# Adaptive visits in the stick-breaking stage: four weight tiles at every second gate tile, with other buffers and first loads

## The chip, the cores and the metric

The kernel runs on one core of one Trainium2 chip. The core has a matrix engine (TensorE, PE in the profile), a vector engine (VectorE, DVE), a scalar engine (ScalarE, ACT), GpSimd (POOL) and SyncE (SP), which here only issues loads. Sixteen DMA engines move data between the chip's memory and the on-chip SBUF; PE writes its sums into eight banks of PSUM. Each engine works through its own instructions in order and waits on semaphores for the others. The metric is the device time of one execution in microseconds.

## The reference

One step of an encoder layer, for a prompt of 1024 rows and a sample of 32 rows with 512 cached rows:

```python
ada = jax.nn.silu(c) @ w_ada + b_ada
sh1, sc1, gt1, sh2, sc2, gt2 = [a[:, None, :] for a in jnp.split(ada, 6, axis=-1)]
h = rms_norm(x, g_pre_mix) * (1 + sc1) + sh1
q_nope, q_rope, c_kv, k_rope, q_b, k_b, v_b, g_a, g_b = mixer_inputs(h, pos, w_in, g_q_lat, w_uq, g_kv_lat)
...
o_a = sweep_query_blocks(mla_attend, (q_nope, q_rope), pos, (k_nope, k_rope, v_a), pos)
o_b = sweep_query_blocks(sb_attend, (q_b,), pos, (k_b, v_b), pos)
...
merged = (g_a * (o_a.reshape(B, T, H_A * DV) @ w_proj_a)
          + g_b * (o_b.reshape(B, T, H_B * D_HB) @ w_proj_b))
x = x + gt1 * rms_norm(merged @ w_out, g_post_mix)
h2 = rms_norm(x, g_pre_ffn) * (1 + sc2) + sh2
f, new_conv = conv_ffn(h2, conv_state, w_up, conv_w, conv_b, w_down)
x = x + gt2 * rms_norm(f, g_post_ffn)
```

`sb_attend` is the stick-breaking attention: a score matrix, a softplus, a cumulative sum from the right, an exponential, and the product with the values, strictly causal. The adaptive product `silu(c) @ w_ada` has two rows on its left side (prompt and sample) and 1024 x 6144 weights. Its first two sixths are needed for `h`, at the start; the other four (gate 1, shift 2, scale 2, gate 2) only later.

## The kernel before

The stages run one after the other: `stage_h` (norm, first two sixths of the adaptive product), `stage_qkv`, `stage_sb` (stick-breaking attention), `stage_lat` and `stage_mla` (latent attention), `stage_merge`, `stage_up`, `stage_down`. The change lies in `stage_sb` (line 1106) and what it calls.

**The stage.** Four passes, `p` = 0 to 3, each over one pair of heads. What PE, ACT and DVE do in a pass, and in which order, is written out by hand in the string `ORDER`; the loop of `sb_attend` (line 713) reads it token by token, and the order of the tokens is the order on each engine. `S` is a block of scores on PE into a PSUM bank (`S2.0a`: query pair 2, first of two, part a; pairs 0 to 3 are the first head, 4 to 7 the second). `a`, `e`, `l` and `E` are ACT's absolute value, exponential, logarithm and last exponential; `x`, `c`, `k` and `d` are DVE's maximum and sum, cumulative sum, copy and difference. `d` is the last to read the bank, which a later `S` takes over; there are three such banks. `T` turns finished blocks on PE, `h` (ACT) and `v` (DVE) split them into a high and a low part, `V` multiplies them with the values on PE, `o` and `p` bring the result out.

**What fills PE.** The sixteen weight tiles of gates A and B run in between (`gates`, line 1043), four in each pass. A gate tile is three blocks of 352 columns; a block is eight steps, and the token `f` is one step (three matmuls, lines 75 to 77). `G` copies a finished block out of its bank (ACT, line 1080, two buffers `nat`), and GpSimd stores it (line 1081). `W` (ACT) and `w` (DVE) split the next tile's weights, which SP loads when a tile begins.

**The adaptive product.** The last four sixths are 32 weight tiles of 128 x 1024. `ada_step` (line 228) is a visit: for each of `n` tiles four matmuls (line 236), each into 32 rows of one PSUM bank of the tag `mm`, that the gates use too. Before, `n` is 2, and a visit stands behind the first block of each gate tile, as two further `f` steps: sixteen visits, four a pass, which are called the first to the fourth visit here. In the third of a pass a score block, `S6.1b`, stands between the two tiles. The visit's sum is added to an accumulator on DVE (line 244, token `D`), and the next two tiles are fetched (`ada_fetch`, line 218) into the pool `att` (`self.sm2`, tag `A`, five buffers). After eight tiles a sixth is complete: PE turns it (`ada_turn`, line 250) behind the second block of the gate tile, and token `Q` puts it away. The very first two tiles are fetched at the start of the stage into the pool `sb` (`S`), between the loads of the first head's Q and K and those of its V.

**Queues.** All loads of the stage go through SP in the order of the program: `load` (line 83) chains each to the one before. Behind the first loads come the next gate tile's weights (`wr`), then the second head's Q and K (token `S2.0a`), its V (`S2.1a`), and from `S3.1b` and `V3.0` on those of the next pass. The caches of the sample rows (`sample_load(1)`) are loaded at the last gate tile. Stores and the bias rows of the adaptive product go through GpSimd.

Of the kernel before, what the change touches and what calls it, by code (L numbers as in the profile page):

```python
# [8 lines left out]
F32 = mybir.dt.float32  # L9
# [8 lines left out]
P = 128  # L18
D = 1024
KT = 8  # L20
TP = 1024
# [11 lines left out]
BIG = 1056  # L33
# [11 lines left out]
class K:  # L45
# [182 lines left out]
    def ada_step(self, n, pool, tp, late):  # L228


        nc, a = self.nc, self.a
        ps = self.bank("mm")
        for i, (v, k) in enumerate(self.ada_todo[:n]):
            w = self.ada_w.pop(0)
            for j in range(4):
                nc.tensor.matmul(ps[32 * j : 32 * j + 32, :256], self.cT[:, k], w[:, j * 256 : j * 256 + 256],
                                 start=i == 0, stop=i == n - 1)
            if i < n - 1:
                yield
        if v > 2 and self.ada_todo[0][1] == 0:  # L240
            self.acc = self.tl(tp, [P, 256], F32, "ada")
            self.ada_bias(v)
        acc = self.acc
        late.append(lambda: nc.vector.tensor_tensor(acc, acc, ps[:, :256], ALU.add))
        del self.ada_todo[:n]
        self.ada_fetch(n, pool)
        self.ada_sum = v if k == KT - 1 else None
        yield

    def ada_turn(self):  # L250

# [192 lines left out]
    def stage_qkv(self):  # L444
# [245 lines left out]

    ORDER = """
        S0.0 S0.1 a0.0 S1.0 a0.1 e0.0 e0.1 l0.0 f2 l0.1 x0.0 a1.0 x0.1 f1 c0.1 c0.0 e1.0 f1 l1.0 f1 d0.0 d0.1
        E0.0 f1 x1.0 c1.0 E0.1 f1 S1.1 S2.0a a1.1 T0.0 d1.0 f1 G a2.0a h0.0 v0.0 f1 e2.0a f1 e1.1 S2.0b l2.0a D
        f2 l1.1 x2.0a V0.0 E1.0 c2.0a f1 a2.0b o0 f1 x1.1 e2.0b f1 W p0 f1 k2.0a d2.0a l2.0b f1 c1.1 E2.0a f1
        S2.1a x2.0b G f1 a2.1a d1.1 e2.1a c2.0b f2 E1.1 f1 w l2.1a S2.1b f1 a2.1b x2.1a T1.1 e2.1b T1.0 d2.0b
        h1.1 c2.1a f1 h1.0 f1 l2.1b v1.1 S3.0a E2.0b v1.0 f1 a3.0a f1 k2.1a d2.1a G e3.0a x2.1b V1.1 E2.1a c2.1b
        l3.0a S3.0b V1.0 x3.0a a3.0b o1 f1 p1 T2.2 h2.2 e3.0b d2.1b f1 c3.0a f1 E2.1b f1 l3.0b v2.2 S3.1a k3.0a
        d3.0a T2.1 h2.1 a3.1a x3.0b E3.0a V2.2 f1 c3.0b T2.0 e3.1a S3.1b h2.0 f1 v2.1 l3.1a f1 G v2.0 a3.1b f1
        x3.1a W f1 d3.0b V2.1 c3.1a D V2.0 f1 w o2 S4.0 e3.1b E3.0b f1 a4.0 f1 l3.1b f1 p2 e4.0 k3.1a d3.1a l4.0
        f2 x3.1b E3.1a f1 x4.0 c3.1b f1 G T3.3 c4.0 S4.1 a4.1 T3.2 h3.3 d3.1b f1 e4.1 v3.3 h3.2 f1 d4.0 f1 l4.1  # L700
        E3.1b v3.2 S5.0 f1 E4.0 x4.1 c4.1 a5.0 V3.3 e5.0 V3.2 l5.0 d4.1 T3.1 E4.1 x5.0 T3.0 h3.1 f1 c5.0 h3.0
        S5.1 S6.0a v3.1 a5.1 f1 v3.0 a6.0a T4.0 e5.1 f1 d5.0 h4.0 V3.1 E5.0 v4.0 f1 l5.1 V3.0 G x5.1 S6.0b e6.0a
        f1 o3 c5.1 f1 a6.0b l6.0a e6.0b f1 p3 l6.0b d5.1 f2 x6.0b E5.1 V4.0 x6.0a f1 o4 c6.0a S6.1a T5.1 p4
        a6.1a T5.0 k6.0a d6.0a h5.1 f1 c6.0b e6.1a f1 G h5.0 v5.1 f1 E6.0a v5.0 S6.1b l6.1a f1 W f1 x6.1a d6.0b
        V5.1 V5.0 D c6.1a E6.0b a6.1b S7.0a w o5 f2 e6.1b l6.1b a7.0a f1 k6.1a p5 e7.0a f1 d6.1a x6.1b E6.1a f1
        c6.1b l7.0a S7.0b f1 x7.0a T6.2 a7.0b f1 d6.1b h6.2 c7.0a f1 E6.1b f1 G e7.0b S7.1a v6.2 f1 k7.0a d7.0a
        l7.0b T6.1 T6.0 a7.1a h6.1 V6.2 x7.0b c7.0b h6.0 S7.1b e7.1a f1 v6.1 E7.0a f1 v6.0 l7.1a f1 d7.0b a7.1b
        f1 x7.1a V6.1 E7.0b V6.0 e7.1b c7.1a f1 G o6 l7.1b f1 p6 k7.1a d7.1a x7.1b f2 E7.1a f1 c7.1b f2 T7.3
        d7.1b T7.2 h7.3 f1 h7.2 E7.1b v7.3 f1 G f1 v7.2 f1 V7.3 V7.2 D T7.1 f1 h7.1 v7.1 T7.0 f1 h7.0 v7.0 f1
        V7.1 f2 V7.0 f1 o7 f1 W p7 f1 Q f1 w G f7 G  # L710
    """.split()

    def sb_attend(self, score, V, out, fill, then):
        nc = self.nc
        act, vec = nc.scalar.activation, nc.vector
        tiles, banks, seen = {}, {}, {}
        common = self.sums(V, out, tiles)
        todo = None
        for x in self.ORDER:
            if todo:  # L720
                todo()
            todo = then.get(x)
            k, x = x[0], x[1:]
            if k in "fGDQWw":
                for _ in range(int(x or 1)):
                    fill(k)
                continue
            h, u = divmod(int(x[0]), 4)
            if k in "SaelxckdE":
                n, i, part = x[0], int(x[2]), x[3:]  # L730
                w = (2 * u + i + 1) * P
                m = w // 2 if part else w
                c0 = m if part == "a" else 0
                if k == "S":
                    if part != "b":
                        tiles[x[:3]] = self.tl(self.At, [P, TP], F32, "A")
                    banks[x] = self.tl(self.ps, [P, 512], F32, "s")
                    score(h, banks[x], 2 * u + i, c0, max(m, 256))
                    continue
                ps, A = banks[x][:, :m], tiles[x[:3]][:, c0 : c0 + m]  # L740
                if k == "a":
                    act(A, ps, AF.Abs)
                elif k == "e":
                    act(A, A, AF.Exp, scale=-1.0)
                elif k == "l":
                    act(A, A, AF.Ln, bias=1.0)
                elif k == "x":
                    vec.scalar_tensor_tensor(A, ps, 0.0, A, ALU.max, ALU.add)
                elif k == "c":
                    r = A[:, ::-1]  # L750
                    if part == "b":
                        vec.tensor_tensor_scan(r, r, r, seen[x[:3]], ALU.add, ALU.bypass)
                    else:

                        vec.tensor_tensor_scan(r, self.reset[:, 512 - m : 512][:, ::-1], r, -NEG, ALU.mult, ALU.add)
                elif k == "k":
                    seen[x[:3]] = self.tl(self.sm, [P, 1], F32, "mn")
                    vec.tensor_copy(seen[x[:3]], A[:, 0:1])
                elif k == "d":
                    vec.tensor_tensor(A, ps, A, ALU.subtract)  # L760
                else:
                    act(A, A, AF.Exp)  # L762
                continue
            common(k, x, h, u)
# [278 lines left out]
    def gates(self):  # L1043
# [7 lines left out]
        def steps():  # L1051
            for m in range(16):
                wh, wl = w.pop(0)
                for b, (c0, n) in enumerate(self.BLK):
                    if b == 0:
                        c = 2208 + (m + 1) * P if m < 15 else 3 * P
                        raw.append(self.wload([(0, 1024, self.a["w_in"][0, :, c : c + P].rearrange("(k p) c -> p k c", p=P), 8)]))
                    ps.append((m, c0, n, self.bank("mm")))
                    for k in range(KT):
                        self.mm3(ps[-1][3][:, :n], wh[:, k], wl[:, k], self.Hh[k][:, c0 : c0 + n],  # L1060
                                 self.Hl[k][:, c0 : c0 + n], k == 0, k == KT - 1)
                        if k < KT - 1:
                            yield
                    if b == 1 and self.ada_sum is not None:
                        ada.append(self.ada_turn())
                    yield
                    if b == 0:
                        yield from self.ada_step(2, self.sm2, self.Sp, ada)
                        if m == 15:
                            self.sample_load(1)  # L1070

        step = steps()

        def do(kind):
            if kind == "f":
                next(step)
            elif kind == "G":
                m, c0, n, x = ps.pop(0)
                g = self.tl(self.At, [P, 512], F32, "nat")
                nc.scalar.copy(g[:, :n], x[:, :n])  # L1080
                nc.gpsimd.dma_start(self.gd[m, :, c0 : c0 + n], g[:, :n])
            elif kind in "DQ":
                ada.pop(0)()
            elif kind == "W":
                w.append((self.tl(self.W, [P, 1024], F32R, "wh"), self.tl(self.W, [P, 1024], F32R, "wl")))
                self.hi(w[0][0], raw[0])
            else:
                self.lo(w[0][1], raw.pop(0), w[0][0])
                w[0] = tuple(v(x) for x in w[0])
# [16 lines left out]
    def stage_sb(self):  # L1106
# [35 lines left out]
            self.tl(S, [P, TP], F32, "A")  # L1142
        first(0)
        self.sm2 = self.tc.alloc_tile_pool(name="att", bufs=2, reuse_waits="tile")

        self.sent = self.wlast
        queries(0, 0)
        self.ada_w = []
        self.ada_fetch(2, S)
        values(0, 0)  # L1150

        def score(h, ps, i, c0, n):
# [5 lines left out]
        E = mybir.EngineType  # L1158
        for p in range(4):
            then = {"S2.0a": lambda: queries(p, 1), "S2.1a": lambda: values(p, 1)}  # L1160
            if p < 3:
                then.update({"S3.1b": lambda: queries(p + 1, 0), "V3.0": lambda: values(p + 1, 0)})
            with self.tc.manual_schedule(engines={E.PE, E.Activation, E.DVE}):
# [1443 lines left out]
```

## Time and profile before

| What | Value |
|---|---|
| Runs, median (lowest to highest) | 1707.84 us (1705.19 to 1708.3), 3 runs |
| Profiled execution, its own time | 1706.82 us |
| Its span, first to last instruction | 1704.7 us |
| Mean granted PE clock | 0.994 |
| Matmuls of the adaptive visits (line 236) | 256 records, 18.2 us busy |
| DVE additions of the visits (line 244) | 16 of about 0.41 us |

How to read the views: times are microseconds from the span's start. In the timeline a row is start, duration, engine, line, operation, tile written and tiles read, shape and count of merged instructions; a bracket at its end is the idle time of the engine before the row and what ended it. Matmuls are pipelined, so the distance from one start to the next tells what one costs, rather than its duration. An fp32 matmul of a visit leaves two records, so a tile of four matmuls has eight. A row of an SP or POOL DMA is its issue, not the transfer. In a view by stretch there stand, behind the stretch and its length, the busy time and instruction count of each engine, PE's granted clock, the share of the DMA engines' time and the GB/s moved.

### The profile page before, as it was taken

How to read it: one execution, taken by the hardware profiler on the slowest of the kernel's cores; microseconds unless marked ns; L12 is line 12 of the kernel's file. 1: busy time of each engine (PE TensorE's matmuls, PEld its weight loads, DVE VectorE, ACT ScalarE, POOL GpSimd, SP SyncE). 2: the span in 40 equal slices, each digit the busy share in tenths (PEclk: the TensorE clock that was granted, in tenths of full speed). 3: DMA queues.
4: the chain of work that ended last, by engine and by line, in shares of the span. 5: the costliest groups of instructions: out<-in, count | busy, mean ns of one | idle time of the engine just before them, and what ended most of it. 6: DMA issues, size and time to landing. Idle time of an engine off the chain costs nothing. (4 is left out here: it accounts for less than half of the span.)

```text
span 1704.7 us, 30268 instructions
## 1 busy us (share of the span) xinstructions
PE 1660.8 (97%) x11646; PEld 1512.1 (89%) x11646; DVE 1272.9 (75%) x2129; ACT 993.6 (58%) x1945; POOL 292.8 (17%) x569
## 2 busy tenths in 40 slices
PE   5999999999999999999999999999999999999997
PEld 3999889999999898998889789999999999887885
DVE  4865697979783688777766779887787777787456
ACT  4544597978774667777763476444444444544442
POOL 3113311111110221111100221221121111110013
PEclk8999999999999999999999999999999999999999
DMA  9345984647432421222374531433333333697643
GB/s 333 100 133 180 280 250 130 200 117 227 150 104 66 149 79 47 67 68 70 107 238 140 173 131 62 134 104 131 131 104 132 131 108 133 231 331 250 207 139 120
DMA packets 185728, 255.20 MB, mean 150 GB/s; under 512 B 14702, under 2 KB 125056, under 8 KB 185584
## 3 DMA queue, kind: packets, MB, share of 16 engines
q1 hardware_dynamic: 164944, 194.11, 36.5%
q0 software_dynamic: 20416, 59.08, 9.8%
q8 instruction: 91, 1.49, 0.4%
q14 instruction: 53, 0.43, 0.1%
q10 hardware_dynamic: 224, 0.09, 0.0%
HBM read 187.86 MB, written 64.57 MB: 148 GB/s over the span
## 5 line engine op out<-in xcount | busy, mean ns | idle before, releaser
L68 ACT ACTIVATE wh<-wr 128x1024 fp32r<-128x1024 f32 (+5 forms) x163 | 132.2, 820 | 226.3 <-PE s L2061 80.4
L71 DVE TENSOR_TENSOR wl<-wr,wh 128x1024 fp32r<-128x1024 f32 (+5 forms) x163 | 149.9, 928 | 78.0 <-ACT wh L68 77.6
L75 PE MATMUL mm<-hh,wh 128*128 128x352 f32 x456 | 153.0, 336 | 0.0
L76 PE MATMUL mm<-hl,wh 128*128 128x352 f32 x456 | 149.5, 328 | 0.4 <-DVE hl L331 0.3
L77 PE MATMUL mm<-hh,wl 128*128 128x352 f32 x456 | 148.7, 326 | 0.0
L2060 PE MATMUL mm<-T,wh 128*128 128x256 f32 (+1 forms) x376 | 108.1, 288 | 0.0
L2062 PE MATMUL mm<-T,wl 128*128 128x256 f32 (+1 forms) x376 | 107.0, 285 | 0.3 <-DVE wl L71 0.2
L2061 PE MATMUL mm<-T,wh 128*128 128x256 f32 (+1 forms) x376 | 106.7, 284 | 0.0
L2060 PE MATMUL s<-T,wh 128*128 128x256 f32 (+1 forms) x348 | 99.2, 285 | 0.0
L2062 PE MATMUL s<-T,wl 128*128 128x256 f32 (+1 forms) x348 | 99.1, 285 | 0.0
L2061 PE MATMUL s<-T,wh 128*128 128x256 f32 (+1 forms) x348 | 99.0, 284 | 0.0
L71 DVE TENSOR_TENSOR wl<-S,wh 128x1024 fp32r<-128x1024 f32 (+1 forms) x55 | 59.1, 1077 | 49.2 <-ACT wh L68 48.8
L76 PEld LDWEIGHTS mm<-hl,wh 128*128 128x128 f32 x456 | 86.4, 190 | 3.3 <-DVE hl L331 1.8
L75 PEld LDWEIGHTS mm<-hh,wh 128*128 128x128 f32 x456 | 86.4, 190 | 3.2 <-ACT A L762 1.6
L2201 DVE SCALAR_TENSOR_TENSOR u<-u,c,u 128x1058 f32<-128x1058 f32 x68 | 87.0, 1316 | 2.0 <-ACT u L2198 0.7
L77 PEld LDWEIGHTS mm<-hh,wl 128*128 128x128 f32 x456 | 86.5, 190 | 0.2
L803 PE MATMUL tr<-c,A 128*128 128x128 f32 x576 | 84.2, 275 | 0.9 <-DVE A L919 0.3
L68 ACT ACTIVATE wh<-S 128x1024 fp32r<-128x1024 f32 (+1 forms) x55 | 51.8, 943 | 49.5 <-PE s L2061 13.4
L2062 PE MATMUL tr<-T,wl 128*128 128x272 f32 (+1 forms) x272 | 77.6, 285 | 0.2 <-DVE wl L71 0.2
L2060 PE MATMUL tr<-T,wh 128*128 128x272 f32 (+1 forms) x272 | 77.7, 286 | 0.0
L2061 PE MATMUL tr<-T,wh 128*128 128x272 f32 (+1 forms) x272 | 77.3, 284 | 0.0
L71 DVE TENSOR_TENSOR PTl<-tr,PTh 128x512 fp32r<-128x512 f32 x96 | 64.5, 683 | 13.1 <-ACT PTh L68 12.3
(760 smaller groups left out, 5789.2 us busy)
## 6 DMA issues: line engine op xcount, KB each, us to landing
wr<-in_w_up_dram SPq DMA_DIRECT2D x44, 512.0 KB, 4.0
dr<-in_w_down_dram SPq DMA_DIRECT2D x43, 512.0 KB, 5.9
wr<-in_w_in_dram SPq DMA_DIRECT2D x33, 512.0 KB, 5.4
A<-in_w_ada_dram SPq DMA_DIRECT2D x32, 512.0 KB, 7.6
wr<-gdn SPq DMA_DIRECT2D x30, 512.0 KB, 5.0
gdn<-u POOLq DMA_DIRECT2D x23, 512.0 KB, 5.1
gd<-nat POOLq DMA_DIRECT2D x48, 176.0 KB, 4.1
t<-gd SPq DMA_DIRECT2D x16, 528.0 KB, 5.6
```

The source lines that it names most:

```text
L68: self.nc.scalar.activation(out, in_, AF.Identity, scale=scale)
L71: return self.nc.vector.tensor_tensor(out, full, hi.bitcast(F32), ALU.subtract)
L75: m(ps, lh, rh, start=start, stop=False)
L76: m(ps, lh, rl, start=False, stop=False)
L77: self.pe = m(ps, ll, rh, start=False, stop=stop).ins
L803: self.nc.tensor.transpose(tr[:, (2 * s + q) * P : (2 * s + q + 1) * P], at[q][:, b * P : b * P + P], self.idt)
L2060: m(ps[:, :n], w[0][:, k], x[0][:, k, c], start=first and k == 0, stop=False, skip_group_check=True)
L2061: m(ps[:, :n], w[0][:, k], x[1][:, k, c], start=False, stop=False, skip_group_check=True)
L2062: i = m(ps[:, :n], w[1][:, k], x[0][:, k, c], start=False, stop=k == 3, skip_group_check=True)
L2201: nc.vector.scalar_tensor_tensor(y, u[:, w : w + YW], self.cvT[:, w, cc : cc + 1], y, ALU.mult, ALU.add)
```

## The change

A visit takes four tiles, and there are two a pass, at the places of the former second and fourth visits. The visit is a token of its own, `A`, and no longer part of the gate steps, so a pass has 96 steps in place of 104; the order of all other tokens is unchanged, but for the two remaining `D`, which stand later. In the third visit's place the `S6.1b` stays. The stage's first tiles, now four, are fetched behind the second head's V in the first pass and go to the pool `att`; that pool's three `big` buffers and two of its `A` buffers are laid out at the start. The caches of the sample rows are loaded behind the last visit.

```diff
     def ada_step(self, n, pool, tp, late):
...
                 nc.tensor.matmul(ps[32 * j : 32 * j + 32, :256], self.cT[:, k], w[:, j * 256 : j * 256 + 256],
                                  start=i == 0, stop=i == n - 1)
-            if i < n - 1:
-                yield
...
         self.ada_sum = v if k == KT - 1 else None
-        yield
```

`ORDER`, cut to the places that change (line breaks left out):

```diff
-G a2.0a h0.0 v0.0 f1 e2.0a f1 e1.1 S2.0b l2.0a D f2 l1.1
+G a2.0a h0.0 v0.0 e2.0a e1.1 S2.0b l2.0a f2 l1.1
...
-f1 G v2.0 a3.1b f1 x3.1a W f1 d3.0b V2.1 c3.1a D V2.0 f1 w o2 S4.0 e3.1b E3.0b f1 a4.0 f1 l3.1b f1 p2
+f1 G v2.0 a3.1b A x3.1a W d3.0b V2.1 c3.1a V2.0 f1 w o2 S4.0 e3.1b E3.0b f1 a4.0 f1 l3.1b f1 D p2
...
-f1 G h5.0 v5.1 f1 E6.0a v5.0 S6.1b l6.1a f1 W f1 x6.1a d6.0b V5.1 V5.0 D c6.1a
+f1 G h5.0 v5.1 E6.0a v5.0 S6.1b l6.1a W f1 x6.1a d6.0b V5.1 V5.0 c6.1a
...
-v7.3 f1 G f1 v7.2 f1 V7.3 V7.2 D T7.1 f1 h7.1 v7.1 T7.0 f1 h7.0 v7.0 f1 V7.1 f2 V7.0 f1 o7 f1 W p7 f1 Q
+v7.3 f1 G A v7.2 V7.3 V7.2 T7.1 f1 h7.1 v7.1 T7.0 f1 h7.0 v7.0 f1 V7.1 f1 D f1 V7.0 f1 o7 f1 W p7 f1 Q
```

```diff
     def gates(self):
...
-                    if b == 0:
-                        yield from self.ada_step(2, self.sm2, self.Sp, ada)
-                        if m == 15:
-                            self.sample_load(1)
...
+            elif kind == "A":
+                self.ada_step(4, self.sm2, self.Sp, ada)
+                if not self.ada_todo:
+                    self.sample_load(1)
...
     def stage_sb(self):
...
         self.sm2 = self.tc.alloc_tile_pool(name="att", bufs=2, reuse_waits="tile")
+        for g, w, n in (("big", BIG, 3), ("A", TP, 2)):
+            for _ in range(n):
+                self.tl(self.sm2, [P, w], F32, g)
 
         self.sent = self.wlast
         queries(0, 0)
-        self.ada_w = []
-        self.ada_fetch(2, S)
+        self.ada_w, self.ada_sum = [], None
         values(0, 0)
...
             then = {"S2.0a": lambda: queries(p, 1), "S2.1a": lambda: values(p, 1)}
+            if p == 0:
+                then["S2.1a"] = lambda: (values(p, 1), self.ada_fetch(4, self.sm2))
```

More of the change, by code (lines that the diff above doesn't have):

```diff
@@ L692 @@
         S0.0 S0.1 a0.0 S1.0 a0.1 e0.0 e0.1 l0.0 f2 l0.1 x0.0 a1.0 x0.1 f1 c0.1 c0.0 e1.0 f1 l1.0 f1 d0.0 d0.1
[L693 to L696, printed above, removed]
+        E0.0 f1 x1.0 c1.0 E0.1 f1 S1.1 S2.0a a1.1 T0.0 d1.0 f1 G a2.0a h0.0 v0.0 e2.0a e1.1 S2.0b l2.0a f2 l1.1
+        x2.0a V0.0 E1.0 c2.0a f1 a2.0b o0 f1 x1.1 e2.0b f1 W p0 f1 k2.0a d2.0a l2.0b f1 c1.1 E2.0a f1 S2.1a
+        x2.0b G f1 a2.1a d1.1 e2.1a c2.0b f2 E1.1 f1 w l2.1a S2.1b f1 a2.1b x2.1a T1.1 e2.1b T1.0 d2.0b h1.1
+        c2.1a f1 h1.0 f1 l2.1b v1.1 S3.0a E2.0b v1.0 f1 a3.0a f1 k2.1a d2.1a G e3.0a x2.1b V1.1 E2.1a c2.1b
         l3.0a S3.0b V1.0 x3.0a a3.0b o1 f1 p1 T2.2 h2.2 e3.0b d2.1b f1 c3.0a f1 E2.1b f1 l3.0b v2.2 S3.1a k3.0a
-        d3.0a T2.1 h2.1 a3.1a x3.0b E3.0a V2.2 f1 c3.0b T2.0 e3.1a S3.1b h2.0 f1 v2.1 l3.1a f1 G v2.0 a3.1b f1
-        x3.1a W f1 d3.0b V2.1 c3.1a D V2.0 f1 w o2 S4.0 e3.1b E3.0b f1 a4.0 f1 l3.1b f1 p2 e4.0 k3.1a d3.1a l4.0
-        f2 x3.1b E3.1a f1 x4.0 c3.1b f1 G T3.3 c4.0 S4.1 a4.1 T3.2 h3.3 d3.1b f1 e4.1 v3.3 h3.2 f1 d4.0 f1 l4.1
+        d3.0a T2.1 h2.1 a3.1a x3.0b E3.0a V2.2 f1 c3.0b T2.0 e3.1a S3.1b h2.0 f1 v2.1 l3.1a f1 G v2.0 a3.1b A
+        x3.1a W d3.0b V2.1 c3.1a V2.0 f1 w o2 S4.0 e3.1b E3.0b f1 a4.0 f1 l3.1b f1 D p2 e4.0 k3.1a d3.1a l4.0 f2
+        x3.1b E3.1a f1 x4.0 c3.1b f1 G T3.3 c4.0 S4.1 a4.1 T3.2 h3.3 d3.1b f1 e4.1 v3.3 h3.2 f1 d4.0 f1 l4.1
         E3.1b v3.2 S5.0 f1 E4.0 x4.1 c4.1 a5.0 V3.3 e5.0 V3.2 l5.0 d4.1 T3.1 E4.1 x5.0 T3.0 h3.1 f1 c5.0 h3.0
@@ L703 @@
         f1 o3 c5.1 f1 a6.0b l6.0a e6.0b f1 p3 l6.0b d5.1 f2 x6.0b E5.1 V4.0 x6.0a f1 o4 c6.0a S6.1a T5.1 p4
[L704 to L710, printed above, removed]
+        a6.1a T5.0 k6.0a d6.0a h5.1 f1 c6.0b e6.1a f1 G h5.0 v5.1 E6.0a v5.0 S6.1b l6.1a W f1 x6.1a d6.0b V5.1
+        V5.0 c6.1a E6.0b a6.1b S7.0a w o5 f2 e6.1b l6.1b a7.0a f1 k6.1a p5 e7.0a f1 d6.1a x6.1b E6.1a f1 c6.1b
+        l7.0a S7.0b f1 x7.0a T6.2 a7.0b f1 d6.1b h6.2 c7.0a f1 E6.1b f1 G e7.0b S7.1a v6.2 f1 k7.0a d7.0a l7.0b
+        T6.1 T6.0 a7.1a h6.1 V6.2 x7.0b c7.0b h6.0 S7.1b e7.1a f1 v6.1 E7.0a f1 v6.0 l7.1a f1 d7.0b a7.1b f1
+        x7.1a V6.1 E7.0b V6.0 e7.1b c7.1a f1 G o6 l7.1b f1 p6 k7.1a d7.1a x7.1b f2 E7.1a f1 c7.1b f2 T7.3 d7.1b
+        T7.2 h7.3 f1 h7.2 E7.1b v7.3 f1 G A v7.2 V7.3 V7.2 T7.1 f1 h7.1 v7.1 T7.0 f1 h7.0 v7.0 f1 V7.1 f1 D f1
+        V7.0 f1 o7 f1 W p7 f1 Q f1 w G f7 G
     """.split()
@@ L723, in sb_attend @@
             k, x = x[0], x[1:]
-            if k in "fGDQWw":
+            if k in "fGDQWwA":
                 for _ in range(int(x or 1)):
```

## The prediction

> **What bounds the kernel now.** I read the page, then busy times by stretch inside one pass of the stick-breaking stage, then the timelines of PE, ACT and DVE there, and last the start of the stage with its DMA queues. The page says that PE is the bound:
>
> ```profile
> PE 1660.8 (97%) x11646; PEld 1512.1 (89%) x11646; DVE 1272.9 (75%) x2129; ACT 993.6 (58%) x1945; POOL 292.8 (17%) x569
> ```
>
> That is an average over stages. The change acts between 186 and 520 us, where a pass (one pair of heads) takes 79.4 us; I take the third pass, 364 to 443.4 us. By stretch (length, then busy us and instructions of PE, PEld, DVE, ACT and POOL, clock, DMA share, GB/s):
>
> ```profile
> 364.00:376.80 12.80, 12.47 (x90) 11.63 (x90) 11.53 (x22) 12.36 (x29) 2.14 (x4) 1.00 0.11 35
> 376.80:405.50 28.70, 28.62 (x205) 26.70 (x209) 27.74 (x49) 25.53 (x57) 3.86 (x8) 1.00 0.56 160
> 405.50:423.70 18.20, 18.07 (x124) 16.13 (x123) 17.63 (x31) 16.32 (x33) 2.76 (x5) 1.00 0.87 264
> 423.70:443.40 19.70, 19.64 (x144) 18.43 (x148) 10.63 (x20) 9.74 (x23) 2.21 (x4) 1.00 0.69 202
> ```
>
> In the first and third stretch ACT (12.36 of 12.80) and DVE (17.63 of 18.20) are full too; in the fourth they are half idle and PE alone sets the pace. So the question is which engine ends last just behind each visit. PE:
>
> ```profile
> 363.50 0.32 PE L76 MATMUL mm<-hl,wh 128*128 128x352 f32 x1
> 363.67 0.32 PE L77 MATMUL mm<-hh,wl 128*128 128x352 f32 x1
> 363.92 1.07 PE L236 MATMUL mm<-A,cT 128*32 128x256 f32 x16
> 364.92 0.41 PE L1154 MATMUL s<-KH,Q 128*128 128x320 f32 x1
> ...
> 376.81 0.47 PE L1154 MATMUL s<-KH,Q 128*128 128x448 f32 x1 [0.34 <-DVE A L760]
> ...
> 405.44 0.64 PE L236 MATMUL mm<-A,cT 128*32 128x256 f32 x8
> 406.01 0.44 PE L1154 MATMUL s<-KH,Q 128*128 128x384 f32 x1
> ```
>
> and ACT (the last bracket is the idle time before the row and what ended it), then DVE:
>
> ```profile
> 364.03 0.45 ACT L1080 COPY nat<-mm 128x352 f32<-128x352 f32 x1 [0.51 <-PE mm L77]
> ...
> 405.55 0.45 ACT L1080 COPY nat<-mm 128x352 f32<-128x352 f32 x1 [0.46 <-PE mm L77]
> ...
> 437.70 0.45 ACT L1080 COPY nat<-mm 128x352 f32<-128x352 f32 x1 [3.67 <-PE mm L77]
> ```
>
> ```profile
> 365.71 0.41 DVE L244 TENSOR_TENSOR ada<-ada,mm 128x256 f32<-128x256 f32 x1
> 366.47 0.49 DVE L748 SCALAR_TENSOR_TENSOR A<-s,A 128x320 f32<-128x320 f32 x1 [0.35 <-ACT A L746]
> ...
> 408.18 0.41 DVE L244 TENSOR_TENSOR ada<-ada,mm 128x256 f32<-128x256 f32 x1
> 408.50 0.95 DVE L755 TENSOR_TENSOR_SCAN A<-reset,A 128x384 f32<-128x384 bf16 x1
> ```
>
> The reader is to see a hand-over. At 364.03 ACT starts on the last gate matmul *ahead of* the first visit. From there it runs without a pause, hands to DVE at 366.47, and DVE ends the wait of S3.0b on PE at 376.81. The visit at 363.92 is on PE beside that chain and not in it. After 376.81 PE leads until ACT waits for it at 405.55, just beside the third visit; then ACT and DVE lead again. From the fourth visit on PE leads (ACT idle 3.67 us at 437.70).
>
> **The change, part by part.** The price of a visit first. The two-tile visit at 363.92 takes 1.00 us to the next start; the third visit is split by S6.1b, and its one tile takes 0.57 us (405.44 to 406.01). So a further tile costs 1.00 - 0.57 = 0.43 us, and an entry 0.57 - 0.43 = 0.14 us, plus 0.08 at its edge, where PE needs 0.25 us from 363.67 to 363.92 in place of the 0.17 us before it: 0.22 us. Now 16 visits have 20 entries; after the change there are 8 with 8.
>
> *First visit of each pass removed.* PE reaches S3.0b some 1.1 us sooner (1.00 and the edge) and waits there that much longer, about 1.4 us in place of 0.34: worth nothing. Its DVE addition goes too (365.71), but DVE then waits for ACT until 366.47 anyway: nothing. The cover is the ACT-DVE chain; without it the removal would be worth 1.1 us a pass.
>
> *Third visit removed.* PE again outruns DVE, so its 1.3 us (two entries of 0.57 and edges) are worth nothing by themselves. But the addition at 408.18 stands in a dense DVE stretch; the next instruction starts 0.32 us behind it, and so the chain ends 0.32 us sooner: -0.32 us a pass.
>
> *Second and fourth visits hold four tiles.* Each is 2 x 0.43 = 0.86 us longer. The second lies in the stretch 376.8 to 405.5, where PE is busy 28.62 of 28.70 us: bounds 0 (DVE's 27.74 us would allow it to absorb all but some) and 0.86; I take 0.86, since ACT still waits for PE at its end, 405.55. The fourth lies where ACT idles 3.67 us behind it: 0.86. Their DVE additions stay as many, later by a few gate steps; the transposes of the sum come more than a gate block behind the second one of a pass, with DVE half idle: nothing.
>
> A pass gains 0.86 + 0.86 - 0.32 = 1.40 us; four passes 5.6 us.
>
> [...]
>
> *The first loads.* At the stage's start two adaptive tiles go out ahead of V and of the next gate weights:
>
> ```profile
> 186.31 0.86 SPq L83 DMA_DIRECT2D A<-in_w_ada_dram  x2
> 187.28 0.58 SPq L83 DMA_DIRECT2D V<-vd  x1
> 187.98 1.90 SPq L83 DMA_DIRECT2D wr<-in_w_in_dram  x1
> ```
>
> ```profile
> 186.00:212.00 26.00, 22.86 (x158) 0.93 1.05 344
> ```
>
> ```profile
> 203.10 0.45 ACT L1080 COPY nat<-mm 128x352 f32<-128x352 f32 x1 [0.44 <-PE mm L77]
> ...
> 210.12 1.06 ACT L68 ACTIVATE wh<-wr 128x1024 fp32r<-128x1024 f32 x1 [2.59 <-DMA wr<-in_w_in_dram]
> ...
> 217.15 0.46 ACT L1080 COPY nat<-mm 128x352 f32<-128x352 f32 x1
> ```
>
> ```profile
> 199.94 0.64 PE L1154 MATMUL s<-KH,Q 128*128 128x512 f32 x1 [2.49 <-DVE A L760]
> ...
> 212.71 0.44 PE L1154 MATMUL s<-KH,Q 128*128 128x384 f32 x1 [1.36 <-DVE A L760]
> ...
> 218.05 0.47 PE L1154 MATMUL s<-KH,Q 128*128 128x448 f32 x1 [0.35 <-DVE A L760]
> ```
>
> The DMA engines are full there (share 1.05, 344 GB/s), and 2 x 512 KB at 344 GB/s are 3.05 us, more than the 2.59 us that ACT waits for those weights. Without them ahead the wait should go, and with it PE's 1.36 us. Upper bound of the gain: the stretch from ACT's copy to S3.0b is 218.05 - 203.10 = 14.95 us here and 376.81 - 364.03 = 12.78 us in the third pass, so 2.17 us. What is late next is the third gate copy (217.15): it needs the buffer of the first, whose store was issued late and landed slowly:
>
> ```profile
> 208.11 0.57 POOL L1081 DMA_DIRECT2D gd<-nat  x1
> ```
>
> ```profile
> gd<-nat POOLq DMA_DIRECT2D x1, 176.0 KB, 8.9
> ```
>
> 208.11 + 8.9 = 217.0, and the copy would like to start some 2.2 us sooner than 217.15. If the store lands no sooner, nearly nothing is gained; S3.0b, however, does not wait for that copy. Bounds 0 and 2.17; I take 1.5, nearer the upper, since S3.0b is ahead of what the copy holds up.
>
> *Other moved steps.* Four tiles of 512 KB are now asked for at a time into five buffers, so three of these loads wait on SP for the visit's own matmuls, and behind them queue the next gate weights and the second head's Q and K. After the fourth visit these are not needed for the rest of its stretch (19.7 us), and 2 MB at 344 GB/s are 6.1 us; after the second, V of the next pair waits for PE longer than that anyway. Cover gone, 6.1 us each. In the first pass four tiles (before: two) stand ahead of the second gate weights, but 3.05 us less stand ahead of them: even, bounds -3.05 and +3.05. The caches of the sample rows are loaded later, behind the last visit, with nearly a whole fourth stretch (19.7 us) before PE turns them: nothing; without that cover, 1 MB, 3.05 us, once. Buffers laid out ahead of the stage have no instructions: nothing.
>
> **Sum.** 5.6 - 1.5 = +4.1 us. The profiled execution took 1706.82 us (span 1704.7 and 2.1 around it): 1710.9. The median of the runs, 1707.84, lies 1.0 above it, so 1711.9, said as 1712. With the term of the start at its ends (0 and 2.17), and the second visit losing a quarter of a us a pass to slack, it runs from 1710 to 1713.5. A measurement of this kernel cannot tell 0.2%, 3.4 us, from no change; the forecast lies just outside.
>
> **Rivals.**
> 1. *Entries count everywhere (faster).* If PE set the pace behind the first and third visits too, twelve entries of 0.22 us (-2.7) and the start (-2.2) would all be saved: 1707.84 - 4.9 = 1703. For it: PE at 97%, idle 0.6 us a pass. Against it: the wait of 0.34 us at 376.81 is already there with the visit in place. It decides as soon as ACT reaches S3.0b's bank over 1.1 us sooner than now.
> 2. *The clock drops.* Longer waits may cost PE its clock. The 2.49 us before 199.94 were followed by a matmul of 0.64 us, the 1.36 us before 212.71 by none slowed like that; the new wait, about 1.4 us, is close to the latter. The clock of 0.93 over 26 us is 1.8 us lost; four times 7.3: 1719. [...]
> 3. *Absorbed.* If DVE sets the pace in the second stretch and, past the turn, in part of the fourth, the longer visits cost little: 5.6 - 4 x 0.86 - 1.5 = +0.7, 1708.5.
> 4. *Loads late.* ACT waits for the second gate weights in the first pass: +3.05, 1715.
>
> **How the numbers follow.** Forecast 0.63, rival 1 0.14, rival 2 0.07, rival 3 0.12, rival 4 0.04. The range 1706 to 1716 leaves out most of rivals 1 and 2; the forecast's own is 1710 to 1713.5. Slower by over 0.2% (above 1711.2): two thirds of the forecast, with 2 and 4, 0.54. Faster: rival 1, 0.14. Within: 0.32.
>
> **What would show it.** After: PE's wait at S3.0b about 1.4 us in each pass, a wait of about 1 us at S7.0b (the one that the third visit's place hid), visits of 32 records that take 1.87 us, a pass of 80.8 us in place of 79.4, and no ACT wait for weights at 207 us. Wrong would be: a pass of under 79.4 us (the chain past the first visit does run over PE), matmuls slowed behind S3.0b, or an ACT wait at the second or third set of gate weights.

## The result, and the profile after

The changed kernel takes 1713.32 us (median of 8 runs, 1712.18 to 1718.84) against 1707.2 (8 runs of the kernel before on the same chip, 1703.88 to 1710.57). The ratio of the times is 1.0042, with a 95% interval of 1.0028 to 1.0056: slower by 5 to 10 us. (It is not the quotient of the two medians, which is 1.0036, a difference of 6.1 us.) The profiled execution took 1714.6 us, its span is 1712.8.

The page's engine line hardly changes; the time is found only by stretch.

```profile
PE 1662.0 (97%) x11646; PEld 1514.4 (88%) x11646; DVE 1271.4 (74%) x2121; ACT 993.6 (58%) x1945; POOL 295.1 (17%) x569
```

ACT copies twelve gate blocks in a pass, always at the same places of the program. The starts of these copies are therefore marks at which passes of different kernels can be laid side by side. Here are four stretches of the third pass, cut at the copies beside the first, second and third visit's places and one behind the third. The columns are length, then busy us and instructions of PE, PEld, DVE, ACT, POOL, then PE's clock, the DMA share and GB/s. First the kernel before:

```profile
364.03:384.13 20.10, 19.76 (x140) 18.37 (x143) 18.73 (x34) 18.93 (x42) 2.73 (x5) 1.00 0.11 35
384.13:405.55 21.42, 21.36 (x159) 19.97 (x157) 20.56 (x37) 18.96 (x44) 3.27 (x6) 1.00 0.71 201
405.55:414.64 9.09, 8.99 (x64) 7.54 (x64) 8.80 (x16) 8.28 (x17) 1.10 (x2) 1.00 1.05 367
414.64:443.43 28.79, 28.70 (x205) 27.00 (x207) 19.45 (x35) 17.79 (x40) 3.86 (x7) 1.00 0.69 189
```

The changed kernel, the same four:

```profile
367.46:387.54 20.08, 19.17 (x124) 17.97 (x128) 18.38 (x33) 18.83 (x43) 2.73 (x5) 1.00 0.25 73
387.54:409.77 22.23, 22.16 (x173) 20.81 (x173) 20.80 (x37) 18.77 (x44) 3.29 (x6) 1.00 0.81 241
409.77:418.54 8.77, 8.26 (x48) 7.23 (x47) 8.46 (x15) 8.12 (x18) 1.11 (x2) 1.00 0.53 164
418.54:448.21 29.67, 29.51 (x217) 27.40 (x215) 19.38 (x35) 17.79 (x40) 3.88 (x7) 1.00 0.66 178
```

The first visit is gone and its stretch is as long as before (20.08 for 20.10). The second stretch is 0.81 longer, the third 0.32 shorter, the fourth 0.88 longer: 1.35 us a pass. In the first and third stretch PE now has idle time (19.17 busy of 20.08, 8.26 of 8.77); in the other two it is full. The waits and visits themselves, on PE:

```profile
367.90 0.41 PE L1153 MATMUL s<-KH,Q 128*128 128x320 f32 x1 [0.48 <-DVE A L757]
...
380.25 0.47 PE L1153 MATMUL s<-KH,Q 128*128 128x448 f32 x1 [0.45 <-DVE A L757]
...
387.43 1.93 PE L236 MATMUL mm<-A,cT 128*32 128x256 f32 x32
389.29 0.38 PE L814 MATMUL pv<-PTh,V 128*128 128x256 f32 x1
...
412.53 0.47 PE L1153 MATMUL s<-KH,Q 128*128 128x448 f32 x1 [0.40 <-DVE A L757]
```

The start of the stage, on ACT:

```profile
204.74 0.45 ACT L1073 COPY nat<-mm 128x352 f32<-128x352 f32 x1 [3.42 <-DMA qh<-T]
...
209.08 1.05 ACT L68 ACTIVATE wh<-wr 128x1024 fp32r<-128x1024 f32 x1
...
217.51 0.45 ACT L1073 COPY nat<-mm 128x352 f32<-128x352 f32 x1 [1.29 <-DMA gd<-nat]
```

ACT no longer waits for the second gate weights (209.08). In place of that 2.59 us there is a wait of 3.42 us at the first gate copy, for the store of a finished query tile (`qh<-T`), with which the copy has no data in common, and one of 1.29 us at the third copy. S3.0b, on PE, does not come later for it:

```profile
217.52 0.47 PE L1153 MATMUL s<-KH,Q 128*128 128x448 f32 x1 [0.45 <-DVE A L757]
```

Two such stores go out. Their time from issue to landing, minimum, median and maximum, before and after:

```profile
DMA to landing us min/median/max: 6.2/6.3/6.5
```

```profile
DMA to landing us min/median/max: 7.3/8.2/9.0
```

The first head's Q and K are asked for near 180 us in both kernels. The second head's come next behind V and the gate weights, and here the kernels differ, now that the adaptive tiles no longer stand ahead of all these. SP, before and after:

```profile
189.99 5.32 SPq L83 DMA_DIRECT2D Q<-qh  x1
195.74 5.42 SPq L83 DMA_DIRECT2D KH<-kh  x2
```

```profile
189.21 1.79 SPq L83 DMA_DIRECT2D Q<-qh  x1
191.05 1.24 SPq L83 DMA_DIRECT2D KH<-kh  x2
```

Q is asked for 0.8 us sooner, K 4.7 us, and the last of these loads (`KL`) 8.6 us, at 193.23 in place of 201.85; 0.45 us of each is this execution's coming earlier to the stage. So all of them are now asked for before the second of the query tile's stores, which is issued at 195.68.

Last, the turn from the first to the second pass, ACT, before and after:

```profile
284.61 0.45 ACT L1080 COPY nat<-mm 128x352 f32<-128x352 f32 x1 [0.51 <-PE mm L77]
```

```profile
286.74 0.45 ACT L1073 COPY nat<-mm 128x352 f32<-128x352 f32 x1 [1.09 <-DMA gd<-nat]
```

**Where the time went.** Measured from copy to copy, the last of them at 517.17 us before and 523.19 after, the stage is 6.02 us later: 0.70 at the start (from PE's 2.5 us wait near 199.5 to the fourth gate copy 26.09 in place of 25.39 us), 0.59 at the turn (the distance of two copies is 6.31 in place of 5.72), 1.29, 1.30, 1.35 and 1.24 in the four passes, less 0.45 by which this execution came earlier to the stage. The other 2.1 us between the two spans come later, behind the last copy. That part of the span is 1187.5 us before and 1189.6 after, and from 1186.7 to 1190.3 in the thirteen traces of this case, shortest in a kernel that loads the caches of the sample rows late too. So nothing of the change shows in it.

### The profile page after: what moved, and what is told of

Same layout as the page of the kernel before. It is cut to its first block, busy times and chain, and to the rows that moved or that the text cites. A ratio compares the mean times of both kernels' runs of the same rounds, so it can differ in the third digit from the quotient of the medians.

```text
span 1712.8 us, 30258 instructions
## 1 busy us (share of the span) xinstructions
PE 1662.0 (97%) x11646; PEld 1514.4 (88%) x11646; DVE 1271.4 (74%) x2121; ACT 993.6 (58%) x1945; POOL 295.1 (17%) x569
```

## The experiments

The distances below are from copy to copy as above. "Start" is the distance from PE's 2.5 us wait near 199.5 to the fourth gate copy: 25.39 us before. Ratios are to runs of the kernel before on the same chip.

**Visits back, one by one.** In the next three runs passes two to four get visits back; buffers, first loads and first pass stay changed. `places` says at which places of a pass the token `A` stands, `sizes` how many tiles each visit takes, in order; for all four visits:

```diff
+        self.sizes = [4, 4, 2, 2, 2, 2, 2, 2, 2, 2, 2, 2, 2, 2]
...
+            self.places = [[2, 4], [1, 2, 3, 4], [1, 2, 3, 4], [1, 2, 3, 4]][p]
```

> In passes two to four there are again four visits of two tiles at the old places (the third one unsplit); the buffers, the first loads and the first pass are those of the changed kernel. Theory: the three passes lose their +1.3 us each, and the second pass its wait for a late store (0.6): 1713.3 - 3.9 - 0.6 = 1708.8. Rival (the loss sits in the buffers and first loads): 1713. Rival (entries cost, 0.22 us each, everywhere): above the changed kernel by 6 entries x 0.22 = 1.3, so 1714.6.

1709.93 us, ratio 1.0027 (1.0016 to 1.0038). The last pass has the old length: 20.10, 21.44 and 9.09 us for the first three stretches. Between the two ratios lie 2.6 us, less than the 4.5 expected but within what their intervals leave; the profiled execution lost 2.2 us at the start (28.26 against 26.09), of which more below. From the fourth copy to the last its stage is 3.91 us shorter than that of the changed kernel. The rest of the 4.5 went in the third pass, whose third stretch is 9.75 us long in place of 9.09: ACT waits there 1.22 us for gate weights (at 412.98).

The first place alone, `[1, 2, 4]` with 2, 2 and 4 tiles:

> The changed kernel with one visit back: in passes two to four two tiles stand at the first place again, so the second place has two and the fourth keeps four. Theory (a visit at the first place lies beside the chain of scalar and vector engine and costs nothing; at the second place each tile costs 0.43 us): the stretch from the gate copy to S3.0b stays 12.8 us, the second stretch falls from 29.5 to 28.7, the pass from 80.7 to 79.9; three passes -2.5 us, about 1710.8. Rival (entries cost everywhere): an entry more, +0.2 a pass, 1714.

1712.1 us, ratio 1.0024 (1.0013 to 1.0035). First and second stretch of the third pass:

```profile
368.58:388.65 20.07, 19.73 (x140) 18.31 (x144) 18.70 (x34) 18.92 (x42) 2.72 (x5) 1.00 0.25 71
388.65:410.10 21.45, 21.41 (x157) 20.22 (x157) 20.59 (x37) 18.94 (x44) 3.27 (x6) 1.00 0.81 246
```

The visit is back on PE (140 instructions in place of 124), the stretch is not longer, and the second stretch has lost the 0.8 us. So the theory, and not the count of entries; it is the stretches that decide this, as the whole times lie too near each other. The third place alone, `[2, 3, 4]` with 4, 2 and 2 tiles:

> The changed kernel with the other removed visit back: in passes two to four two tiles stand at the third place, here behind S6.1b, so the fourth place has two and the second keeps four. Theory: -0.87 at the fourth place, +0.33 in the third stretch for the vector engine's addition; the pass falls from 80.7 to 80.2, three passes -1.6 us, about 1711.7. Rival (the matrix engine's 1.2 us of the visit count at the third place): +0.35 a pass, 1714.4. Second rival, from the run with the visits at the first and third places (what hurts at the third place is the score block S6.1b behind the visit): the stretch does not grow, since S6.1b is ahead of the visit here.

1713.57 us, ratio 1.0034 (1.0023 to 1.0044).

```profile
410.92:420.00 9.08, 8.73 (x64) 7.52 (x63) 8.78 (x16) 8.28 (x17) 1.10 (x2) 1.00 1.05 381
420.00:448.77 28.77, 28.64 (x201) 26.87 (x199) 19.45 (x35) 17.79 (x40) 3.87 (x7) 1.00 0.65 172
```

The third stretch grows by 0.31, not by the visit's 1.2, and not by nothing; the fourth loses 0.90. Whether PE or DVE makes those 0.31 the next run decides, with DVE work alone:

```diff
-V5.1 V5.0 c6.1a
+V5.1 V5.0 + + c6.1a
...
+            elif kind == "+":
+                nc.vector.tensor_tensor(self.acc, self.acc, self.acc, ALU.max)
```

> The changed kernel with two more operations on the vector engine and nothing on the matrix engine, at the place of the third visit's former addition: twice the maximum of the accumulator with itself (128 x 256, the values stay). Theory (the third stretch goes at the pace of the vector engine): the stretch from the third gate copy to the fourth visit grows by the length of the two, 0.6 to 0.8 us a pass, four passes 2.4 to 3.2 us. Rival (the vector engine has slack there, and the third stretch shrank by 0.33 us for the matrix engine's sake): no change.

1717.74 us, ratio 1.0059 (1.0042 to 1.0077). The third stretch, and in it DVE:

```profile
412.29:421.85 9.56, 8.24 (x48) 7.21 (x47) 9.22 (x17) 8.29 (x18) 1.10 (x2) 1.00 0.48 150
```

```profile
414.91 0.88 DVE L1079 TENSOR_TENSOR ada<-ada 128x256 f32<-128x256 f32 x2
415.71 0.95 DVE L751 TENSOR_TENSOR_SCAN A<-reset,A 128x384 f32<-128x384 bf16 x1
```

The two hold the scan up by 415.71 - 414.91 = 0.80 us, and the stretch grows by 9.56 - 8.77 = 0.79. PE has 48 instructions there as in the changed kernel. DVE sets that stretch's pace.

**The start.** Two kernels move the gate-copy buffers to the front of their pool, away from the memory in which the stored query tile lies; the second gives them three buffers:

```diff
-        for g, w, n in (("PTh", 512, 2), ("PTl", 512, 2), ("o", 256, 2), ("nat", 512, 2)):
+        for g, w, n in (("nat", 512, 3), ("PTh", 512, 2), ("PTl", 512, 2), ("o", 256, 2)):
```

> The changed kernel, with the gate-copy buffers nat laid where they no longer share memory with the tile whose spill is stored at the start of the stage; still two of them. Theory (the first gate copy's wait of 3.42 us at 204.7 is for that spill, and behind it the third copy waits for the first one's store): the first copy starts at about 202 to 203, the wait at the third copy grows from 1.3 to 2.5 to 3.5 us, and S3.0b of the first pass (217.5) comes 0 to 2 us sooner: 1711.5 to 1713. Rival (the start is bound by the 344 GB/s of the transfers, not by that buffer): the first copy waits less but the stage's second gate tile starts when it does now: 1713.3.

1712.28 us, ratio 1.0045 (1.0031 to 1.006). The gate copies on ACT:

```profile
201.18 0.45 ACT L1073 COPY nat<-mm 128x352 f32<-128x352 f32 x1 [1.68 <-DMA vd<-sg]
...
217.05 0.45 ACT L1073 COPY nat<-mm 128x352 f32<-128x352 f32 x1 [4.39 <-DMA gd<-nat]
```

The first copy comes 3.0 us behind PE's wait in place of 5.25, but the third then waits 4.39 us for the first one's store: the wait only moved, as the theory had it, by more than the 3.5 us expected. PE then waits 2.86 us at 218.44, and its clock is 0.66 over the 5 us from there. The start is 27.75 us, and nothing is gained.

> As the kernel with the gate-copy buffers laid apart, and three of them in place of two. Theory (both waits at the start and the one of the second pass, 1.1 us at 286.7, are for these buffers): all three go, S3.0b of the first pass comes about 2 us sooner than the 217.5 of the changed kernel, and the second pass gains 0.6 us: 1713.3 - 2.6 = 1710.7. Rival (transfers bind the start): as the changed kernel, 1713.

1711.54 us, ratio 1.0031 (1.0019 to 1.0043).

```profile
203.17 0.45 ACT L1073 COPY nat<-mm 128x352 f32<-128x352 f32 x1 [1.46 <-PE mm L77]
...
214.59 0.45 ACT L1073 COPY nat<-mm 128x352 f32<-128x352 f32 x1
```

Both waits for transfers are gone, and the one at 286.74 too (the distance there is 5.76). The start is 223.24 - 199.98 = 23.26 us, 2.13 less than before the change. To see which part the buffers alone have in this, the kernel before got the same edit:

> The kernel before, with three gate-copy buffers laid apart in place of two. It asks which part of the start's gain in the run with three buffers comes from the buffers and which from the moved first loads. Theory (the wait for the second gate weights, 2.59 us at 210.1, is for transfers): with the first loads left ahead of them, that wait stays, the fourth gate copy comes at 225.3 as before, and the time is the same. Rival (the buffers alone do it): the fourth gate copy at 223.2, and 2 us under the kernel before.

1706.09 us, ratio 1.0001 (0.9992 to 1.001). The wait for the weights stays:

```profile
207.89 1.06 ACT L68 ACTIVATE wh<-wr 128x1024 fp32r<-128x1024 f32 x1 [2.31 <-DMA wr<-in_w_in_dram]
```

Its start is 23.79 us in this one execution, 1.6 less than before, and 1.31 of these come ahead of the first gate copy (201.15 - 199.30 = 1.85 us in place of 203.10 - 199.94 = 3.16), where its gate matmuls behind the 2.5 us wait came every 0.16 us, and not every 0.30 as in the execution before (clock 0.53 over the 2 us from there). So this profile alone doesn't tell the two theories apart; the times say no gain. With that 1.31 taken off, the moved loads are worth 1.8 us (25.10 against 23.26), if the copies have their buffers.

**The start is not the same in every execution.** Five of these kernels have the changed kernel's program up to the fourth gate copy, word for word. Their starts are 26.39, 27.79, 27.96, 28.16 and 28.26 us; with the changed kernel's own 26.09 the mean is 27.44, 2.05 over the one start of before that is on record. Two things differ. In four of the five others the longer of the query tile's stores took 9.7 to 10.2 us, not 9.0, and in all five the first copy came 5.92 to 6.42 us behind PE's wait, not 5.25. And behind that copy PE then waits 2.59 to 3.06 us, and the gate matmuls after the wait come every 0.29 or 0.30 us in all five, with a clock of 0.50 over 5 us in the run shown next; in four of them the way from the first copy to the fourth is 21.80 to 21.89 us, not 20.84 (20.44 in the fifth). The run with all visits back, PE, and its 5 us from there:

```profile
207.92 1.62 PE L832 MATMUL pv<-ptd,V 128*128 128x256 f32 x4 [3.06 <-issue]
209.33 0.49 PE L75 MATMUL mm<-hh,wh 128*128 128x352 f32 x1
209.63 0.49 PE L76 MATMUL mm<-hl,wh 128*128 128x352 f32 x1
```

```profile
207.90:212.90 5.00, 4.89 (x17) 4.65 (x18) 4.26 (x8) 4.81 (x11) 3.09 (x6) 0.50 0.89 210
```

In the changed kernel's profiled execution that wait was 2.16 us, and the matmuls behind it came every 0.16 us, not every 0.30:

```profile
206.01 0.35 PE L814 MATMUL pv<-ptd,V 128*128 128x256 f32 x1 [2.16 <-issue]
...
207.08 0.33 PE L75 MATMUL mm<-hh,wh 128*128 128x352 f32 x1
207.24 0.32 PE L76 MATMUL mm<-hl,wh 128*128 128x352 f32 x1
```

**Other places.** If the first and third places have slack and the second and fourth none, the visits should stand at the former:

```diff
+        self.sizes = [4, 4, 4, 4, 4, 4, 4, 4]
...
+            self.places = [[2, 3], [1, 3], [1, 3], [1, 3]][p]
```

> The visits of four tiles stand at the first and third places in passes two to four (second and third in the first pass); still eight visits, 32 tiles, same buffers and loads. Theory (a visit costs only where the matrix engine leads: at the second and fourth places in full, at the first and third only what is left above the chain of scalar and vector engine): per pass against the kernel before -1.1 -1.1 for the two places emptied, about +0.5 at the first place (0.86 less the 0.34 us it waits there), 0.5 to 0.8 at the third; about -1.1 a pass in three passes, and +0.3 in the first: about 1704, that is 9 us under the changed kernel. Rival (what counts is how many visits and tiles there are, wherever they stand): the same as the changed kernel, 1713. Rival (the loss sits in the buffers and first loads): also 1713.

1734.0 us, ratio 1.0165 (1.0152 to 1.0178): none of the theories. The third and fourth stretch of the second pass:

```profile
334.30:343.39 9.09, 9.09 (x80) 8.06 (x79) 8.78 (x16) 8.18 (x17) 1.38 (x3) 1.00 1.04 341
343.39:377.00 33.61, 28.72 (x189) 26.82 (x191) 19.17 (x33) 17.53 (x40) 5.62 (x11) 1.00 0.42 111
```

The first two stretches are near the theory (20.41 and 21.14 us), the third is better: four tiles cost nothing there (9.09, as before with two, and PE full). The loss sits in the fourth, with no visit in it, 33.61 in place of 28.79, and PE idle for 4.9 of it. PE, and the DVE copy that belongs to the row at 342.45:

```profile
342.45 0.38 PE L253 MATMUL tr<-c,ada 128*128 128x128 f32 x2
344.60 0.60 PE L818 MATMUL tr<-c,A 128*128 128x128 f32 x4
347.44 0.66 PE L818 MATMUL tr<-c,A 128*128 128x128 f32 x4 [2.25 <-DVE PTl L71]
```

```profile
367.61 0.18 DVE L256 COPY c<-tr 128x16 f32<-128x16 f32 x1
```

With eight tiles done at the third place, the turn of the sum (L253) comes at 342.45, while the copy that empties its bank (token `Q`) stays at the pass's end, 25 us later. In between two groups of transposes wait until DVE has read the ones before (2.25 and 1.59 us), and a score block waits 0.96 us. That the held bank is the cause is not shown, as it was not tried by itself; but a run below has the same four tiles at that place, the turn at the end, and no such loss.

> A version that should beat both: three gate-copy buffers laid apart from the spilled tile, the first loads of the changed kernel, and visits of 4, 2 and 2 tiles at the second to fourth places in the first pass and of 3, 1, 2 and 2 in the others (third one behind S6.1b). Theory, against the kernel before: start -2.4 (as in the run with three buffers), first pass +0.8, the others -0.3 each (a tile moved from the second place, 0.43, to the first, which has 0.34 us of slack): about 1704, 0.1 to 0.2% under the kernel before. Rival (the start's gain is lost in later loads, as in the changed kernel): same as before.

1706.86 us, ratio 0.9997 (0.9987 to 1.0007): the rival's number, though not for the rival's reason. First and second stretch of the third pass:

```profile
361.33:381.40 20.07, 20.07 (x148) 18.58 (x152) 18.68 (x34) 18.86 (x43) 2.72 (x5) 1.00 0.11 35
381.40:402.86 21.46, 21.09 (x149) 19.98 (x146) 20.59 (x37) 18.84 (x44) 3.27 (x6) 1.00 0.69 199
```

The third tile at the first place is free, but the tile taken from the second place gives nothing back (21.46; before 21.42): PE idles 0.37 us there instead. The second place is in balance with two tiles: two more cost 0.81 of their 0.86 us, one less saves nothing. The start kept its gain (23.35 us); 0.64 went back in the rest of the stage, in the first pass, where four tiles stand at the second place.

> The same buffers and first loads, with 2, 4 and 2 tiles in the first pass and four visits of two tiles in the others, as in the kernel before. Theory: the start's gain alone, about -2.8 us at the fourth gate copy, less nothing later: 1704. Rival (the start's gain is lost later): the same as the kernel before, 1707.

1704.18 us, ratio 0.9994 (0.9985 to 1.0003). Its start is 23.95, the rest of the stage as before. The expected 2.8 us was read off raw times of the run just above (its last copy is at 514.33, before at 517.17), and 1.44 of it had come ahead of the stage. Measured from PE's wait the start's gain is 25.39 - 23.95 = 1.44 us, within what the runs can tell.

> Three gate-copy buffers laid apart, the first loads of the changed kernel, and the tiles moved to where the runs so far show the matrix engine waiting anyway: 2, 4 and 2 at the second to fourth places in the first pass, 3, none, 4 and 1 at the first to fourth in the others, the third ahead of S6.1b. Theory, from the stretches between gate copies of the runs so far: a pass falls by 0.31 (second place emptied) and 0.43 (a tile less at the fourth) under that of the kernel before, three passes -2.2; the stage ends 5.9 us sooner than before; about 1702. Rival (four tiles at the third place cost their 0.86 us after all): -2.5 in all, 1705.

1702.36 us, ratio 0.9976 (0.9967 to 0.9986): faster than both kernels. The third pass:

```profile
359.73:379.80 20.07, 20.07 (x146) 18.62 (x145) 18.68 (x34) 18.87 (x43) 2.73 (x5) 1.00 0.46 139
379.80:400.94 21.14, 20.90 (x143) 19.61 (x146) 20.28 (x36) 18.90 (x45) 3.29 (x6) 1.00 0.59 155
400.94:410.03 9.09, 9.09 (x79) 8.08 (x78) 8.78 (x16) 8.18 (x17) 1.11 (x2) 1.00 1.06 368
410.03:438.54 28.51, 28.42 (x198) 26.93 (x200) 19.39 (x35) 17.88 (x40) 3.88 (x7) 1.00 0.50 135
```

78.81 us in place of 79.40, with PE full in the first and third stretch: three tiles at the first place and four at the third are hidden, the emptied second place gives 0.28, the single tile at the fourth 0.28 (expected 0.31 and 0.43). With the start (23.29, so -2.10) and -1.76 for the rest of the stage that makes 3.9 us; the ratio says 4.1. The expected 5.9 had the same 1.4 too many, and it had 2.2 us for the passes where 1.76 were measured.

## Why the prediction was right, and where it was not

1712 was predicted, 1713.32 measured, and the mechanism of the passes is shown, by its own terms:

| Term, us | Predicted | Measured | Shown by |
|---|---|---|---|
| First visit removed | 0 | -0.02 | the visit put back alone: 20.07 and 20.08 |
| Second visit, four tiles | +0.86 | +0.81 | two tiles there: 21.45, four 22.23 |
| Third visit removed | -0.32 | -0.32 | DVE work alone: +0.79 for 0.80 |
| Fourth visit, four tiles | +0.86 | +0.88 | two tiles there: 28.77, four 29.67 |
| A pass | +1.40 | +1.24 to 1.35 | |
| First loads | -1.5 | +0.7 (mean of six starts +2.05) | the buffers laid apart |
| Turn of the passes | 0 | +0.59 | three buffers: gone |

*The steps of the passes* hold one by one. Visits of 32 records take 1.86 us (1.87 predicted). The waits at S3.0b and S7.0b came out at 0.45 and 0.40 us, not 1.4 and 1.0: in the first stretch a part of the freed time stands ahead of S2.0b (0.48). PE is 0.45 us ahead of the kernel before there, and small pauses between matmuls leave 0.11 of it at S3.0b. The stretch's length, which the argument rested on, is unchanged.

*The step that failed* is "The first loads": "Bounds 0 and 2.17; I take 1.5, nearer the upper, since S3.0b is ahead of what the copy holds up." S3.0b came 0.1 us sooner (18.03 us behind PE's wait in place of 18.11), and the fourth copy 0.7 later. From the first copy to S3.0b it is 217.52 - 204.74 = 12.78 us in place of 14.95: the whole upper bound of 2.17 was gained, since the wait for the weights did go. But the sum took the start of that stretch, the first copy, as fixed, and it came 2.09 us later behind PE's wait (5.25 in place of 3.16). Behind S3.0b the third copy's wait for the first one's store, named as late next, took 0.78. What had no term, then, was a second thing that the moved loads make late: the store of the query tile, in whose memory the gate-copy buffer lies. (The copy stops waiting for it when the buffer is moved, and the buffers are laid out in the same order in both kernels.) Before, it landed at 196.12 + 6.5 = 202.6, half a us ahead of the copy at 203.10, so the copy did not wait for it. With the moved loads, which have the second head's Q and K asked for up to 8.6 us sooner among full DMA engines (share 1.03 over these 9 us, 1.05 over the 6.5 us in the kernel before), it took 9.0 us. In seven kernels with the moved loads the longer of the two stores takes 9.0 to 10.2 us, in the kernel before 6.5; with three buffers in the kernel before, POOL's wait for that store ends 6.82 us behind its issue, without them 6.75. Which of the moved loads slows it was not tried. The lower bound had to go below nothing, as far as that store could slip. With the buffers apart and three of them the term is -2.13, beyond the 1.5.

*"After the fourth visit these are not needed for the rest of its stretch (19.7 us)"* was true of the loads, and the wrong question: what they made late was a gate copy's store in the same DMA engines, 0.59 us at 286.74. In the 11 us ahead of that copy the DMA share is 1.09, in the kernel before 0.46. In the runs with visits back at all places and at the first, the fourth visit of the first pass asks for two tiles and not four, and the distance is 5.73 and 5.72 us, as before the change.

Two errors of opposite sign thus stood beside each other: the passes 0.4 us too dear, the start and the turn some 3 to 4 us too cheap. The change forecast was +4.1 us, and the medians give 6.1, the interval 5 to 10. That the median of 1713.32 is only 1.3 over the forecast is partly luck: the kernel before came out 0.6 us under the 1707.84 from which the forecast was worked out. And the range to 1713.5 held the result although the term of the start, +0.7, lay outside its bounds (a gain of 0 to 2.17).

*The rivals.* Entries do not count everywhere (with a visit more at the first place the first stretch is 20.07 us long, without it 20.08). Absorbed is wrong for added tiles (0.81 of 0.86) and right for removed ones (21.46 with one tile, 21.42 with two). The loads were not late for the second gate weights. The clock did not drop in the passes of the changed kernel (PE waits of up to 0.5 us, clock 1.00 from 260 to 523.2 us), but at the start it did in some executions (0.50 over 5 us in one), behind a wait that no rival had (2.59 to 3.06 us).

## What to carry to other kernels

Find the marks that every variant of a kernel passes, and compare lengths between marks, not times from the span's start: each term of the sum then shows by itself, and a shift from an earlier stage isn't taken for a gain. Slack was one-sided here: the second place, where PE is in balance with another engine, charged 0.81 us for two tiles added, and paid nothing for one removed (21.46 us, 21.42 before) and 0.28 for two. So the filler belonged where another engine's chain is longer, up to the point at which PE is full: three tiles at the first place and four at the third left their stretches at 20.07 and 9.09 us (20.10 and 9.09 before). And when loads are moved ahead, ask which store lands just in time beside them, and whose buffer lies in the memory that it reads (here one that took 6.5 us took 9.0, and a copy waited 3.42 us for it).

## What the runs showed of the hardware

Waits of PE of the same length were followed by different clocks. In the run with visits at the first and third places the second and the third pass have the same wait of 2.25 us, the second shown above at 347.44, the third here:

```profile
431.70 0.66 PE L818 MATMUL tr<-c,A 128*128 128x128 f32 x4 [2.25 <-DVE PTl L71]
```

In the 2 us from there the granted clock is 1.00 in the second pass and 0.64 in the third:

```profile
347.40:349.40 2.00, 1.96 (x14) 1.87 (x15) 0.63 (x2) 1.26 (x3) 0.00 (x0) 1.00 0.00 0
431.70:433.70 2.00, 2.00 (x10) 1.90 (x11) 0.67 (x2) 1.30 (x3) 0.00 (x0) 0.64 0.03 8
```

So it was with the wait of 2.49 or 2.50 us at the stage's start. From 1.3 to 2.5 us behind it the gate matmuls came 0.29 or 0.30 us apart (from line 76 to line 77) in twelve of the thirteen traces, and 0.16 apart in the kernel before with three buffers. Over the 2 us from that wait the clock is 0.53 in the kernel before and 0.50 in the changed kernel.
